# A two-layer trunk with adaLN on one core: where small loads are queued, at what rate modulation weights are taken in, how norm sums and reciprocals are formed, and what the weight splits queue behind

## The chip, the cores and the metric

One core of a Trainium2 chip runs the whole program. Its engines are TensorE (PE), VectorE (DVE), ScalarE (ACT), GpSimd (POOL) and SyncE (SP). The metric is the device time of one execution in microseconds, as the median of several. Every time below is of the kernel before the change.

## The reference

x is one sequence of 256 tokens with 2048 features, c one conditioning vector of 2048. For each of two layers:

```python
mod = (silu(c) @ ada_w[layer] + ada_b[layer])[:, None, :]          # 2048 -> 6 x 2048
sh_m, sc_m, g_m, sh_f, sc_f, g_f = jnp.split(mod, 6, axis=-1)
hm = rms_norm(x, norm_mix_g[layer]) * (1.0 + sc_m) + sh_m
y = ab_mixer(hm, ...) if layer == 0 else cd_mixer(hm, ...)         # each: one projection in, two mixers, one out
x = x + (1.0 + g_m) * y
hf = rms_norm(x, norm_ffn_g[layer]) * (1.0 + sc_f) + sh_f
x = x + (1.0 + g_f) * swiglu(hf, w_gate, w_up, w_down)             # 5632 wide
```

ab_mixer is a gated MLP over token chunks beside a state space scan (SSD) with a short convolution and a gated RMS norm. cd_mixer is stick-breaking attention on 12 heads beside block attention (MoBA) on 4 heads whose q and k get an RMS norm per head. All is in fp32.

## The kernel before

All activations lie transposed: 128 features on the partitions, 256 tokens along a row, 16 such k-tiles. Weights are streamed once, in slabs of two k-tiles by 512 columns (512 KB): SP issues the transfer of raw (L293, four buffers), ACT rounds it to hi (L295), DVE takes lo = raw - hi (L298), three buffers each. PE multiplies in fp32r three times: h by hi, l by hi, h by lo, where h and l are the same split of the activations. dense_ws (L315) keeps the weights stationary and moves 256 columns (the tokens), dense_as (L351) keeps the activations stationary and moves 512. The product of a whole block of 512 output columns gathers in PSUM (accps).

The modulation c @ ada_w is not made on PE. ada_unit (L194) brings in tiles of ada_w (araw, three buffers, L232; the first 16 tiles are in other buffers), and DVE multiplies each by a column of silu(c) and adds it into acc (L211). Behind the last tile end() sums acc over the partitions by small sel matmuls (L217, recorded at L156) and adds the bias (mod, L220). pump (L272) is called once per slab: it adds a rate (RATES for the three groups below, RATE after) and issues a tile for each whole unit. take (L266) makes the uses of tiles issued some slabs earlier.

The first stage, the projection of layer 0, runs in three groups over k: k-tiles 0 to 3, 4 to 8 and 9 to 15 (GROUPS), each over the same 14 blocks of 512 columns, so 28, 42 and 56 slabs. A group needs the modulation of its own k-tiles only. The first group's modulation is 16 tiles of 128x1024 that are read before any weight. What a group needs is made by gains (gs, L465) and adaln, per k-tile: t on DVE (L457), h on ACT (L459), l on DVE (L460). In the last group each finished block goes on to the convolution, the SSD or the gating (DVE and ACT).

At the start x comes in four tiles; PE turns them (L507), ACT copies them to xT (L508) and sums their squares (L515); the variance goes through a square root on ACT (L404) and a reciprocal of 128x2 on DVE (L405), and two matmuls with the reciprocal as a broadcast operand spread it over all partitions (L408). ACT also issues the small loads (rows of gains, biases and of SSD parameters, L126 to L137, L562, L563, L567), which PE then turns into columns (to_cols).

At the four later norms (before the SSD output, before both FFNs, before layer 1) Ssq gathers squares, total() sums them over the partitions by matmuls with one column (ones), and rstd_bcast (L399) does root, reciprocal and broadcast, with WARM matmuls on ident ahead and behind. Two of the norms, and the start, copy the result from PSUM (keep, L414); the others read it there. The eight MoBA norms (L943 to L950) go the same way without WARM.

The order on each engine comes from a scheduler that goes by priorities (tc.high_priority) and its own timeline; tc.issue_after binds one instruction behind another.

## Time and profile before

| | us |
|---|---|
| Three executions | 2680.24, 2683.21, 2684.34 |
| Median | 2683.21 |
| Profiled execution | 2682.86 |
| Its span in the trace | 2681.1 |
| PE busy (97% of the span) | 2610.5 |
| DVE busy (69%) | 1860.3 |
| ACT busy (46%) | 1235.4 |

A PE that is busy 97% of the span can still run at half clock, and its matmuls overlap in the records. So one reads the granted clock beside the busy time, stretch by stretch, and at each place where PE waits looks for what released it.

### The profile page before, as it was taken

The page shows a single profiled execution, that of the slowest core. Times are in us where ns is not written, and L with a number is a line of the kernel's source. Part 1 is how long each engine was busy: PE and PEld are TensorE (multiplying, and loading weights), DVE is VectorE, ACT ScalarE, POOL GpSimd, SP SyncE. Part 2 cuts the span into 40 slices and gives each one's busy share as a digit, 9 for nine tenths or more (in the row PEclk, how much of TensorE's full clock was granted, in tenths as well). Part 3 has the DMA queues.
Part 4 walks back from the last instruction along what each step waited for, and adds up shares of the span by engine and source line. Part 5 has one row for each costly group of instructions (what it writes and reads, how often), then busy time and mean ns, then how long its engine had stood idle before and what let it go on. Part 6 is the DMA issues. An engine that isn't in the chain of part 4 may idle for free.

```text
span 2681.1 us, 39012 instructions
## 1 busy us (share of the span) xinstructions
PE 2610.5 (97%) x15277; PEld 2301.9 (86%) x15277; DVE 1860.3 (69%) x2085; ACT 1235.4 (46%) x1540; POOL 3.2 (0%) x18
## 2 busy tenths in 40 slices
PE   4989999999999999999999999999999999999999
PEld 4989889999988888888888988999988888888888
DVE  5688997887867788777777777666655454445444
ACT  3533574654445444444444544444444444444443
POOL 0000000000000000000000000000000000000000
PEclk7999999999999999999999999999999999999999
DMA  7988797777879989999988788877466666666664
GB/s 269 294 283 304 235 300 253 214 244 232 294 246 306 307 291 307 305 305 301 302 299 301 227 280 283 277 246 230 152 195 189 189 192 188 189 188 191 189 194 144
DMA packets 303650, 665.79 MB, mean 248 GB/s; under 512 B 23504, under 2 KB 25962, under 8 KB 303466
## 3 DMA queue, kind: packets, MB, share of 16 engines
q1 hardware_dynamic: 300480, 662.79, 77.0%
q8 instruction: 119, 1.95, 0.3%
q10 hardware_dynamic: 2986, 0.51, 0.1%
q14 instruction: 65, 0.53, 0.1%
HBM read 661.12 MB, written 2.10 MB: 247 GB/s over the span
## 4 chain that ended last, share of the span: by engine, by line
PE 92%; DVE 3%; DMA 3%; issue 1%; ACT 1%; SPq 0%; ACTq 0%; DVEq 0%
PE accps L156 57%; PE accps L342 25%; PE pm L156 4%; PE pm L342 4%; PE pm L147 1%; DMA raw<-in_ab_w_in 1%; DMA araw<-in_ada_w 1%; DVE acc L211 1%; DVE lo L298 1%; DVE t L625 0%; ACT hi L295 0%; DVE t L457 0%; DMA t<-in_gm_w_s 0%; DMA blk<-in_x 0%; DMA blk<-in_ada_w 0%
## 5 line engine op out<-in xcount | busy, mean ns | idle before, releaser
L298 DVE TENSOR_TENSOR lo<-raw,hi 128x1024 fp32r<-128x1024 f32 (+1 forms) x878 | 1059.0, 1207 | 696.9 <-ACT hi L295 691.7
L295 ACT ACTIVATE hi<-raw 128x1024 fp32r<-128x1024 f32 (+1 forms) x878 | 917.8, 1046 | 1249.5 <-PE accps L156 817.2
L156 PE MATMUL accps<-hi,h 128*128 128x512 f32 x1664 | 651.1, 391 | 0.6 <-ACT hi L295 0.6
L156 PE MATMUL accps<-hi,l 128*128 128x512 f32 x1664 | 648.6, 390 | 2.3 <-DVE l L460 2.3
L342 PE MATMUL accps<-h,lo 128*128 128x256 f32 x1856 | 503.6, 285 | 7.3 <-DVE lo L298 7.3
L342 PE MATMUL accps<-h,hi 128*128 128x256 f32 x1856 | 504.9, 286 | 5.8 <-ACT h L459 5.2
L342 PE MATMUL accps<-l,hi 128*128 128x256 f32 x1856 | 503.9, 286 | 1.1 <-DVE l L389 0.6
L211 DVE SCALAR_TENSOR_TENSOR acc<-araw,ct,acc 128x1024 f32<-128x1024 f32 (+2 forms) x377 | 465.7, 1235 | 3.8 <-DMA araw<-in_ada_w 3.4
L156 PE MATMUL accps<-lo,h 128*128 128x512 f32 x1664 | 445.9, 390 | 0.4 <-DVE lo L298 0.4
L156 PEld LDWEIGHTS accps<-hi,l 128*128 128x128 f32 x1664 | 312.5, 188 | 67.1 <-DVE l L460 3.2
L156 PEld LDWEIGHTS accps<-hi,h 128*128 128x128 f32 x1664 | 312.5, 188 | 66.2 <-ACT hi L295 1.4
L156 PEld LDWEIGHTS accps<-lo,h 128*128 128x128 f32 x1664 | 311.8, 188 | 66.1 <-DVE lo L298 1.6
L342 PEld LDWEIGHTS accps<-h,hi 128*128 128x128 f32 x1856 | 348.2, 193 | 8.8 <-ACT h L459 6.0
L342 PEld LDWEIGHTS accps<-h,lo 128*128 128x128 f32 x1856 | 346.4, 193 | 10.5 <-DVE lo L298 8.9
L342 PEld LDWEIGHTS accps<-l,hi 128*128 128x128 f32 x1856 | 347.7, 193 | 3.0 <-DVE l L389 0.8
L156 PE MATMUL accps<-hi,blk 128*128 128x512 f32 x1248 | 310.3, 390 | 0.0
L156 PEld LDWEIGHTS accps<-hi,blk 128*128 128x128 f32 x1248 | 233.0, 188 | 47.7
L156 PE MATMUL accps<-lo,blk 128*128 128x512 f32 x624 | 166.9, 389 | 0.0
L156 PEld LDWEIGHTS accps<-lo,blk 128*128 128x128 f32 x624 | 117.1, 188 | 24.4
L342 PE MATMUL pm<-blk,hi 128*128 128x256 f32 x448 | 80.6, 284 | 0.0
L342 PE MATMUL accps<-blk,hi 128*128 128x256 f32 x384 | 69.7, 285 | 0.9 <-ACT blk L388 0.5
L342 PEld LDWEIGHTS pm<-blk,hi 128*128 128x128 f32 x448 | 69.3, 192 | 0.2
(238 smaller groups left out, 1538.7 us busy)
## 6 DMA issues: line engine op xcount, KB each, us to landing
araw<-in_ada_w SPq DMA_DIRECT2D x323, 512.0 KB, 5.4
raw<-in_ffn_w_gate SPq DMA_DIRECT2D x176, 512.0 KB, 4.2
raw<-in_ffn_w_up SPq DMA_DIRECT2D x176, 512.0 KB, 4.5
raw<-in_ffn_w_down SPq DMA_DIRECT2D x176, 512.0 KB, 4.9
raw<-in_ab_w_in SPq DMA_DIRECT2D x130, 512.0 KB, 4.9
raw<-in_cd_w_in SPq DMA_DIRECT2D x96, 512.0 KB, 4.7
raw<-in_ab_w_out SPq DMA_DIRECT2D x64, 512.0 KB, 5.0
raw<-in_cd_w_out SPq DMA_DIRECT2D x32, 512.0 KB, 4.7
```

The costliest lines, as they stand in the source:

```text
L147: T.transpose(dst, src, ident)
L156: return T.matmul(o, a, b, start=first, stop=last, skip_group_check=True)
L211: V.scalar_tensor_tensor(acc, r, ct[nr][:, g:g + 1], acc, op0=OP.mult, op1=OP.add)
L295: A.activation(hi, raw, AF.Copy)
L298: wlast[1] = V.tensor_tensor(lo, raw, hi.bitcast(F32), op=OP.subtract)
L342: T.matmul(acc[n], a[:, n * P:(n + 1) * P], b, start=first and n % 2 == 0, stop=final, skip_group_check=True)
```

## The change

There are six edits. First, ACT issues four small loads at its very front (c twice, the first layer's ada_b, the gains of the mixer norms) and the other small loads, with the narrow weight of dt, are issued by SP behind the first four slabs; their columns are made in block 4 of the first group. Second, RATES is 1.3, 0.92 and 0.3 in place of 0.9, 0.85 and 0.5, and QUIET leaves out the modulation tiles for 8 slabs behind the first adaln of a stage, except in the first stage. Third, rstd_of replaces total and rstd_bcast: matmuls with ones as a 128x128 operand give the sum on all partitions for 256 tokens, and root and reciprocal run on 128x256; the start keeps the old way. WARM goes, except at the start. Fourth, pace: the hi of slab i queues behind the h of k-tile 2i - 1, its lo behind the l of that tile; and each t queues behind the l two tiles ahead of it. Fifth, the tail blocks of dense_ws gather their last two columns tiles in PSUM tiles of their own. Sixth, dense_as makes all h by hi, then l by hi, then h by lo of a slab.

```diff
-WARM = (2, 2, 10)
-RATES = (0.9, 0.85, 0.5)
+QUIET = 8
+RATES = (1.3, 0.92, 0.3)
...
+        nc.scalar.dma_start(rows3[0:96, :], ada_b[0].rearrange("(k p) -> k p", p=P))
+        nc.scalar.dma_start(rows3[96:128, :], norm_mix_g.rearrange("l (k p) -> (l k) p", p=P))
...
+    def load_rows():
+        nc.sync.dma_start(rows1[32:64, :], rowview(norm_ffn_g))
...
+        nc.sync.dma_start(hb[:, 0, :], ssd_dt_bias.partition_broadcast(P))
+        nc.sync.dma_start(hb[:, 1, :], ssd_a_log.partition_broadcast(P))
...
     def pump():
         slab[0] += 1
+        if quiet[0]:
+            quiet[0] -= 1
+            return
...
+            after = pace[2 * npace[0] - 1] if 0 < 2 * npace[0] <= len(pace) else None
+            npace[0] += 1
             hi = stg.tile([P, 1024], F32R, tag="hi", name="hi", bufs=3)[:, 0:nk * ncol]
-            A.activation(hi, raw, AF.Copy)
+            with (tc.issue_after(after[0]) if after else ExitStack()):
+                A.activation(hi, raw, AF.Copy)
...
-            acc = [t[:, i * S:(i + 1) * S] for t in (pm(), pm()) for i in range(2)]
+            two = pm()
+            acc = [two[:, 0:S], two[:, S:2 * S], pm()[:, 0:S], pm()[:, 0:S]]
...
-            for part in range(2):
+            for part in range(3):
...
+                        dense_mm[0] = mm(acc[:, n, :], (bl if part == 1 else bh)[:, cs], (lo if part == 2 else hi)[:, i, :],
...
+    def rstd_of(sqs, scale):
+        ps = pm()
+        for i, t in enumerate(sqs):
+            mm(ps[:, 0:S], ones, t, first=(i == 0), last=(i == len(sqs) - 1))
+        r = tmp.tile([P, S], F32, tag="rb", name="rb", bufs=2)
+        A.activation(r, ps[:, 0:S], AF.Sqrt, bias=eps6, scale=scale)
         V.reciprocal(r, r)
...
+        return r
...
     def adaln(k, rb, gs, sh):
         t = t1()
-        V.scalar_tensor_tensor(t, xt(k), gs, rb, op0=OP.mult, op1=OP.mult)
+        with (tc.issue_after(pace[-2][1]) if len(pace) > 1 else ExitStack()):
+            V.scalar_tensor_tensor(t, xt(k), gs, rb, op0=OP.mult, op1=OP.mult)
...
-        nc.scalar.dma_start(wdt, w_in0[:, DT0:DT0 + HB].rearrange("(k p) n -> p k n", p=P))
+        nc.sync.dma_start(wdt, w_in0[:, DT0:DT0 + HB].rearrange("(k p) n -> p k n", p=P))
```

ACT at the start, from the last Square or the last evictions on to the first h. rs is the root, cols and adab are turned rows, rb the spread reciprocal. Before:

```order
L181 ACTIVATE t1_303<-t1_91 64x32 x4
L135 DMA t1_103<-in_ssd_conv_w 96x128
L143 ACTIVATE cols1_242<-pm_240 128x128
L136 DMA t1_103<-in_ssd_conv_b 24x128
L143 ACTIVATE adab0_246<-pm_244 128x128
L137 DMA t1_104<-in_ada_b 96x128
L563 DMA hb_351<-in_ssd_a_log 128x32
L567 DMA t2_2455<-in_ab_w_in 128x16x32
L404 ACT_TABLE_LOAD
L404 ACTIVATE rs_267<-var0_248,eps6_97 128x2
L416 ACTIVATE rb_273<-pm_270 128x256
L295 ACTIVATE hi_388<-raw_386 128x1024
```

Now:

```order
L506 ACTIVATE t2_280,half_265<-blk_137 128x512
L498 ACTIVATE xT1_128<-pm_200 128x512
L498 ACTIVATE xT1_128<-pm_206 128x512
L498 ACTIVATE xT2_129<-pm_212 128x512
L498 ACTIVATE xT2_129<-pm_218 128x512
L510 ACT_TABLE_LOAD
L510 ACTIVATE rs_283<-var0_264,eps6_104 128x2
L498 ACTIVATE xT3_130<-pm_224 128x512
L498 ACTIVATE xT3_130<-pm_230 128x512
L143 ACTIVATE adab0_262<-pm_260 128x128
L516 ACTIVATE rb_289<-pm_286 128x256
L295 ACTIVATE hi_367<-raw_365 128x1024
```

The five loads between the evictions and the root are gone from there, and the root stands ahead of the last two evictions of xT.

DVE at the end of group 0, around the mod of the second group (acc 128x640 is the second group's sum, acc 128x896 the third's). Before:

```order
L211 SCALAR_TENSOR_TENSOR acc_416<-araw_1242,ct2_298,acc_416 128x640
L298 TENSOR_TENSOR lo_1365<-raw_1361,hi_1363 128x512
L211 SCALAR_TENSOR_TENSOR acc_416<-araw_1245,ct2_298,acc_416 128x640
L211 SCALAR_TENSOR_TENSOR acc_416<-araw_1248,ct2_298,acc_416 128x640
L211 SCALAR_TENSOR_TENSOR acc_416<-araw_1251,ct2_298,acc_416 128x640
L209 TENSOR_SCALAR acc_1254<-araw_1255,ct2_298 128x896
L220 SCALAR_TENSOR_TENSOR mod0_0_112<-pm_1257,adab0_246 128x5
L220 SCALAR_TENSOR_TENSOR mod0_1_113<-pm_1257,adab0_246 128x5
L465 TENSOR_TENSOR gs_0_1_4_1266<-mod0_1_113,cols1_242 128x5
L457 SCALAR_TENSOR_TENSOR t1_1268<-xT1_125,gs_0_1_4_1266,rb_273 128x256
L457 SCALAR_TENSOR_TENSOR t1_1274<-xT1_125,gs_0_1_4_1266,rb_273 128x256
```

Now:

```order
L300 TENSOR_TENSOR lo_1214<-raw_1210,hi_1212 128x1024
L202 TENSOR_SCALAR acc_1127<-araw_1128,ct2_241 128x896
L300 TENSOR_TENSOR lo_1249<-raw_1245,hi_1247 128x1024
L204 SCALAR_TENSOR_TENSOR acc_1127<-araw_1163,ct2_241,acc_1127 128x896
L213 SCALAR_TENSOR_TENSOR mod0_0_115<-pm_1199,adab0_262 128x5
L300 TENSOR_TENSOR lo_1316<-raw_1312,hi_1314 128x1024
L213 SCALAR_TENSOR_TENSOR mod0_1_116<-pm_1199,adab0_262 128x5
L204 SCALAR_TENSOR_TENSOR acc_1127<-araw_1196,ct2_241,acc_1127 128x896
L454 TENSOR_TENSOR gs_0_1_4_1279<-mod0_1_116,adab0_262 128x5
L445 SCALAR_TENSOR_TENSOR t1_1281<-xT1_128,gs_0_1_4_1279,rb_289 128x256
L445 SCALAR_TENSOR_TENSOR t1_1287<-xT1_128,gs_0_1_4_1279,rb_289 128x256
```

Before, the last uses of the second group's tiles stand directly ahead of its mod; now two uses of the third group's tiles and slabs of the first group stand there, and h and l of the tiles come between slabs.

DVE at the second norm, from the last residual to the first l. Before:

```order
L791 SCALAR_TENSOR_TENSOR xT3_127<-pm_7955,mod0_2_114,xT3_127 128x256 x2
L298 TENSOR_TENSOR lo_8327<-raw_8323,hi_8325 128x1024
L211 SCALAR_TENSOR_TENSOR acc_6611<-araw_7934,ct2_298,acc_6611 128x1024
L298 TENSOR_TENSOR lo_8348<-raw_8344,hi_8346 128x1024
L405 RECIPROCAL rs_8229<-rs_8229 128x2
L211 SCALAR_TENSOR_TENSOR acc_6611<-araw_7986,ct2_298,acc_6611 128x1024
L457 SCALAR_TENSOR_TENSOR t1_8254<-xT0_124,gs_0_4_0_8252,pm_8232 128x256
L457 SCALAR_TENSOR_TENSOR t1_8260<-xT0_124,gs_0_4_0_8252,pm_8232 128x256
L457 SCALAR_TENSOR_TENSOR t1_8266<-xT0_124,gs_0_4_0_8252,pm_8232 128x256
```

Now:

```order
L793 SCALAR_TENSOR_TENSOR xT3_130<-pm_7931,mod0_2_117,xT3_130 128x256
L793 SCALAR_TENSOR_TENSOR xT3_130<-pm_7932,mod0_2_117,xT3_130 128x256
L407 RECIPROCAL rb_8198<-rb_8198 128x256
L445 SCALAR_TENSOR_TENSOR t1_8215<-xT0_127,gs_0_4_0_8213,rb_8198 128x256
L445 SCALAR_TENSOR_TENSOR t1_8221<-xT0_127,gs_0_4_0_8213,rb_8198 128x256
L448 SCALAR_TENSOR_TENSOR l0_8218<-t1_8215,mod0_3_118,h0_8217 128x256
L445 SCALAR_TENSOR_TENSOR t1_8227<-xT0_127,gs_0_4_0_8213,rb_8198 128x256
L448 SCALAR_TENSOR_TENSOR l1_8224<-t1_8221,mod0_3_118,h1_8223 128x256
L445 SCALAR_TENSOR_TENSOR t1_8233<-xT0_127,gs_0_4_0_8213,rb_8198 128x256
L300 TENSOR_TENSOR lo_8286<-raw_8282,hi_8284 128x1024
```

The reciprocal is the one on 128x256 and stands directly behind the residual; the uses of modulation tiles are gone from there, and l comes behind the second t.

## Rows read from the trace of the kernel before

**Rows 1.** The page: the engines' busy time, share and instructions; and the group of the weight split's lo on DVE (busy us, mean ns | idle before).

```profile
PE 2610.5 (97%) x15277; PEld 2301.9 (86%) x15277; DVE 1860.3 (69%) x2085; ACT 1235.4 (46%) x1540; POOL 3.2 (0%) x18
...
L298 DVE TENSOR_TENSOR lo<-raw,hi 128x1024 fp32r<-128x1024 f32 (+1 forms) x878 | 1059.0, 1207 | 696.9 <-ACT hi L295 691.7
```

**Rows 2.** Windows of 50 us of the core: length, busy us of PE, PEld, DVE, ACT and POOL (instructions), granted clock, DMA share, GB/s.

```profile
0.00:50.00 50.00, 17.52 (x67) 12.42 (x67) 22.36 (x27) 16.58 (x40) 3.15 (x18) 0.75 0.84 287
100.00:150.00 50.00, 40.94 (x279) 38.82 (x277) 33.38 (x43) 21.21 (x26) 0.00 (x0) 0.90 0.83 271
200.00:250.00 50.00, 50.00 (x353) 46.79 (x352) 47.17 (x48) 18.65 (x20) 0.00 (x0) 1.00 0.98 346
300.00:350.00 50.00, 46.06 (x268) 40.17 (x268) 50.00 (x84) 29.91 (x48) 0.00 (x0) 0.97 0.78 240
400.00:450.00 50.00, 46.47 (x383) 44.87 (x383) 40.68 (x56) 19.21 (x24) 0.00 (x0) 1.00 0.79 251
```

**Rows 3.** The waits of PE over the span: engine, tile and line <- what it waited for: us in total, times, longest us.

```profile
PE pm L156 <- DVE rs L405: 18.0, 1, 18.0
PE pm L156 <- DVE acc L211: 10.2, 2, 6.9
```

**Rows 4.** Timeline of ACT and its queue (ACTq issues transfers): start us, us, what [idle before <- releaser].

```profile
10.71 2.07 ACT L508 ACTIVATE xT<-pm 128x512 f32<-128x512 f32 x4 [6.82 <-DMA t<-in_moba_k_norm_g]
...
26.80 0.32 ACTq L135 DMA_DIRECT2D t<-in_ssd_conv_w  x1
...
29.52 0.32 ACTq L136 DMA_DIRECT2D t<-in_ssd_conv_b  x1
...
30.87 0.32 ACTq L137 DMA_DIRECT2D t<-in_ada_b  x1
...
33.85 0.40 ACTq L567 DMA_DIRECT2D t<-in_ab_w_in  x1
34.28 1.28 ACT L404 ACT_TABLE_LOAD   x1 [4.12 <-DMA raw<-in_ab_w_in]
```

**Rows 5.** Timeline of DVE, and below it of PE, up to the first dense matmul: start us, us, what [idle before <- releaser].

```profile
35.90 0.17 DVE L405 RECIPROCAL rs<-rs 128x2 f32<-128x2 f32 x1 [13.16 <-ACT rs L404]
35.98 2.60 DVE L211 SCALAR_TENSOR_TENSOR acc<-araw,ct,acc 128x1024 f32<-128x1024 f32 x2
38.62 7.89 DVE L211 SCALAR_TENSOR_TENSOR acc<-blk,ct,acc 128x1024 f32<-128x1024 f32 x6
...
46.66 3.54 PE L156 MATMUL pm<-ones,acc 128*128 128x1 f32 x16 [3.23 <-DVE acc L211]
...
52.18 1.22 PE L342 MATMUL accps<-h,hi 128*128 128x256 f32 x4 [1.45 <-ACT h L459]
```

**Rows 6.** The chain that ended last, in order of time, at three places: start us, us, what (DMA: from issue to landing).

```profile
15.02 7.70 DMA araw<-in_ada_w
...
128.22 4.49 DMA araw<-in_ada_w
...
137.15 5.83 DMA araw<-in_ada_w
...
242.08 5.98 DMA araw<-in_ada_w
```

**Rows 7.** The page's DMA issues: transfer, queue and operation, count, KB each, median us from issue to landing.

```profile
araw<-in_ada_w SPq DMA_DIRECT2D x323, 512.0 KB, 5.4
```

**Rows 8.** Timeline of all engines at the end of group 0 (SPq: SP's queue): start us, us, what [idle before <- releaser].

```profile
136.24 1.92 DVE L211 SCALAR_TENSOR_TENSOR acc<-araw,ct,acc 128x640 f32<-128x640 f32 x2
137.15 7.11 SPq L232 DMA_DIRECT2D araw<-in_ada_w  x4
...
140.72 2.30 PE L156 MATMUL pm<-sel,acc 128*128 128x2 f32 x10 [6.92 <-DVE acc L211]
...
145.15 1.22 PE L342 MATMUL accps<-h,hi 128*128 128x256 f32 x4 [2.13 <-ACT h L459]
```

**Rows 9.** Windows of three other stretches, columns as in rows 2.

```profile
138.00:149.00 11.00, 6.15 (x30) 6.06 (x31) 6.08 (x16) 2.10 (x5) 0.00 (x0) 0.53 0.71 237
755.00:760.00 5.00, 5.00 (x16) 2.88 (x16) 3.51 (x4) 0.65 (x2) 0.00 (x0) 0.66 0.73 192
1540.00:1570.00 30.00, 30.00 (x234) 29.11 (x233) 21.30 (x24) 14.97 (x24) 0.00 (x0) 1.00 0.85 282
```

**Rows 10.** Timeline of ACT and PE at the second norm: start us, us, what [idle before <- releaser].

```profile
754.12 0.71 ACT L435 ACTIVATE t<-xT 128x256 f32<-128x256 f32 x2
...
759.62 0.38 ACT L416 ACTIVATE rb<-pm 128x256 f32<-128x256 f32 x1 [3.69 <-PE pm L156]
...
761.11 0.49 PE L156 MATMUL accps<-hi,h 128*128 128x512 f32 x1
...
762.92 0.50 PE L156 MATMUL accps<-hi,l 128*128 128x512 f32 x1 [1.32 <-DVE l L460]
```

**Rows 11.** Durations on DVE by line and form: ns min/median/max, first and last start us, forms.

```profile
L405 DVE RECIPROCAL rs<-rs x13: 156/163/168, 35.9 to 1931.6; 128x2 f32<-128x2 f32 x13
...
L591 DVE RECIPROCAL t<-t x1: 542/542/542, 278.2 to 278.2; 128x64 f32<-128x64 f32 x1
...
L457 DVE SCALAR_TENSOR_TENSOR t<-xT,gs,pm x40: 472/476/482, 760.0 to 1946.4; 128x256 f32<-128x256 f32 x40
```

**Rows 12.** Timeline of PE at the fourth norm: two matmuls of 512 columns on ident, each in two passes.

```profile
1933.33 1.88 PE L156 MATMUL pm<-ident 128*128 128x512 f32 x4
```

More of the change, by code (lines that the diff above doesn't have):

```diff
@@ L156, in mm @@
         return T.matmul(o, a, b, start=first, stop=last, skip_group_check=True)
-    def warm(n, after):
-        with tc.issue_after(after.ins):
-            ps = pm()
-            for t in n if isinstance(n, list) else [ident[:, None, :].to_broadcast([P, 4, P])] * n:
-                mm(ps, ident, t)
     ct, sel = {}, {}
@@ L309, in trunk @@
     later = deque()
+    dense_mm = [None]
     def run_later():
@@ L341, in dense_ws @@
             for n, (a, b, first, final) in order:
-                T.matmul(acc[n], a[:, n * P:(n + 1) * P], b, start=first and n % 2 == 0, stop=final,
-                         skip_group_check=True)
+                dense_mm[0] = T.matmul(acc[n], a[:, n * P:(n + 1) * P], b, start=first and (n % 2 == 0 or n > pair),
+                                       stop=final, skip_group_check=True)
             if done >= min(DEFER, len(ks)):
@@ L395, in xt @@
         return xT[k // 4][:, k % 4, :]
-    bcast = [None]
-    def rstd_bcast(var, eps, scale, after=None):
-        if after is not None:
-            warm(WARM[0], after)
-        r = small(2, "rs")
-        A.activation(r, var, AF.Sqrt, bias=eps, scale=scale)
-        V.reciprocal(r, r)
-        ps = pm()
-        for cc in range(2):
-            last = mm(ps[:, cc * P:(cc + 1) * P], r[:, cc:cc + 1].to_broadcast([P, P]), ident, first=(cc == 0))
-        bcast[0] = last
-        if after is not None:
-            warm(WARM[1], last)
-        return ps[:, 0:S]
-    def keep(rb):
-        t = tmp.tile([P, S], F32, tag="rb", name="rb", bufs=2)
-        A.activation(t, rb, AF.Copy)
-        return t
+    def rstd_of(sqs, scale):
[4 more added lines that the diff above has]
+        A.activation(r, ps[:, 0:S], AF.Sqrt, bias=eps6, scale=scale)
+        V.reciprocal(r, r)
+        return r
     def warm_sqrt(ssq):
@@ L517, in trunk, with later_cols @@
         V.tensor_reduce(var0, half.rearrange("p (c i) -> p c i", c=2), axis=AX.X, op=OP.add)
-        rb0 = keep(rstd_bcast(var0, eps6, 1.0 / D))
-        warm(firsts[WARM[2]:], bcast[0])
-        take()
-    more_cols()
-    load_rows_b()
-    cols2 = to_cols(rows2, "cols2")
-    adab[1] = to_cols(rows4, "adab1")
+        r0 = small(2, "rs")
+        A.activation(r0, var0, AF.Sqrt, bias=eps6, scale=1.0 / D)
+        V.reciprocal(r0, r0)
+        psr = pm()
+        for cc in range(2):
+            last = mm(psr[:, cc * P:(cc + 1) * P], r0[:, cc:cc + 1].to_broadcast([P, P]), ident, first=(cc == 0))
+        rb0 = tmp.tile([P, S], F32, tag="rb", name="rb", bufs=2)
+        A.activation(rb0, psr[:, 0:S], AF.Copy)
+        with tc.issue_after(last.ins):
+            psw = pm()
+            for t in firsts[10:]:
+                mm(psw, ident, t)
+        take()
+    cols = {}
+    def later_cols():
+        with tc.issue_after(dense_mm[0].ins):
+            cols[1] = to_cols(rows1, "cols1")
+            cols[2] = to_cols(rows2, "cols2")
+            adab[1] = to_cols(rows4, "adab1")
     w_in0 = ab_w_in[0]
```

108 lines of the change are left out of this document (48 added, 60 removed).

## The prediction

> **What bounds the kernel now.** I read the page first: PE is busy 2610.5 us of the span of 2681.1 us [rows 1]. The profiled execution took 2682.86 us, 1.8 us more than its span, and lies 0.35 us under the median of the three, so the sum below is made against 2682.86. An edit can gain only where PE stands or runs at a lower clock. The windows of 50 us say where that is [rows 2]: from 0 to 50 PE is busy 17.52 us, from 100 to 150 it is busy 40.94, and 300:350 and 400:450 lose 3.94 and 3.53 while DVE is at 50.00 and 40.68. A window such as 200:250 loses nothing, with DVE at 47.17 and 346 GB/s moved. The waits of PE name the largest releasers [rows 3]: 18.0 us for one reciprocal and 10.2 us for acc. Then I went to each place.
>
> **Start.** ACT's program order is the cause. Five small loads stand ahead of its square root; each is issued only when a transfer ahead of it has landed, so that the first of these issues is at 26.80 and the last at 33.85; then come 1.28 us of table load and the root [rows 4]. DVE's reciprocal waits for that, 13.16 us idle, and behind it in DVE's order stand eight uses of the modulation weights that had landed: 2.60 + 7.89 = 10.5 us. Only then come the sel matmuls at 46.66 (3.54 us) and the first dense matmul at 52.18 [rows 5].
> In the changed order the loads on ACT are four and at the very front, and the root stands behind the squares and six of the evictions. ACT makes its first evictions at 10.71 [rows 4]. Six evictions (0.52 each, 2.07 for four), eight Squares of the same width at 0.6, the table load and the root end by 20 us even one behind the other from there, and nearer to 16 if the Squares begin as each x tile lands. DVE runs at 1.30 us per use, so the 13 uses behind the reciprocal need 16.9 us. Of the 16 weights the ninth landed at 15.02 + 7.70 = 22.7 [rows 6]; the stream's landings are 1.35 us apart (estimate from ACT's issues at 29.52 and 30.87, which each follow one), so the last lands at about 32.2. DVE ends at 33.5 (bound by landings) to 37 (by its own work). The sel matmuls take 3.5, and from there to the first dense matmul it took 52.18 - 50.20 = 2.0. That gives 39 to 42.5; I take 39, because the root's inputs are there long before the last weight. That is **-13 us** (-9 to -15). Two things can take some back: the SSD row that the exponential on ACT needs is now the tenth small load on SP, and that exponential stands ahead of h3; the narrow weight of dt stands ahead of the hi of the fourth slab. The four first slabs land by 32.2 + 4 x 1.35 = 37.6; issued behind these, both loads land at some 44 to 49 us, with 5.4 us to landing as a large one has [rows 7], which is when PE gets to them. I add nothing and leave 3 us in the range.
>
> **End of group 0.** PE runs out of work at 140.72 - 6.92 = 133.8 [rows 8] (28 slabs since 52.18, so 2.9 us each), and the chain there is araw transfers of 4.49 and 5.83 us one behind the other, with a few uses between [rows 6]. Then come the sel matmuls at half clock (2.30 us) and the wait for h (2.13); dense work resumes at 145.15. So the hole is 11.35 us, and the clock, 0.53 in 138:149 [rows 9], is low for some 3 us behind it, which costs half of that. At a rate of 1.3 per slab in place of 0.9, all 32 transfers of group 1's modulation are issued by slab 28 and its sel matmuls stand two slabs ahead of the end of group 0. Each use costs DVE 0.96 us (1.92 for two [rows 8]) and lies under a slab of 2.9 us on PE beside one lo of 1.21 [rows 1]: 1.21 + 1.3 x 0.96 = 2.46. The four transfers issued in a row took 7.11 us [rows 8], or 1.78 each, and 1.3 of them 2.3 us: less than a slab too. Then only the sel matmuls (half of 2.30 at full clock) and a part of the wait for h remain: **-10 us** (0 to -11.5; the upper end is what a slower stream leaves, below).
>
> **End of group 1 and the stretch to 420.** There one araw transfer of 5.98 us [rows 6] ends the wait, and t and h follow; PE idles some 2.5 us and has a stretch at half clock. With group 2's sel matmuls four slabs ahead that is -4. Behind it DVE is full (300:350: 50.00 [rows 2]). Eight narrow uses of 0.96 have gone ahead into group 0, and at 0.3 per slab in place of 0.5 five fewer wide ones of 1.30 stand in group 2: 14 us less DVE work behind 145, where PE lost 7.5 us in the two windows named. I count well under half of this, because the waits are also for conv and for a late weight of the spatial part: -3. Together **-7** (0 to -12).
>
> **The four norms.** Now: matmuls to one column, root, a reciprocal of 2 columns, a broadcast matmul, and a copy out of PSUM at two of them; PE is filled with matmuls on ident. At the second one the last Square ends at 754.83, the first dense matmul is at 761.11 and the next waits 1.32 us for l, until 762.92 [rows 10]. After: five matmuls of 256 columns, root and reciprocal on 128x256. What a reciprocal on 128x256 costs no row shows. The rows give 162 ns at 2 columns and 542 ns at 64 [rows 11]; the line through both gives 1.72 us at 256, and the lower bound is 0.48 us, what t (also 128x256) takes [rows 11]. I take 1.7, since the 64-column row already shows that the time grows with the columns. A sum matmul costs at most 0.47 (two of 512 columns take 1.88 [rows 12]). From the last Square: 0.47 + root 0.4 (a copy of this shape from PSUM is 0.38 [rows 10]) + 1.7 + t 0.48 + h 0.55 = 3.6 us to the first matmul, against 761.11 - 754.83 = 6.3 now at the second. The others gain less: no copy out of PSUM lies in the chain of the third and fourth, and at the first the root followed on other work. But l now comes right behind the second t, so the wait for l shrinks. Against that stands the clock: without matmuls on ident PE idles 3 us. With them the clock still fell at the second norm (0.66 in 755:760 [rows 9]). I take **-2** in all (-8 to +5, with the upper end at 1.75 us more for each).
> The Trainium skill, page "TensorE: Matmul & The Clock Gate", Part 1, says that the throttled clock is the default state and that activity releases it, which speaks against dropping the matmuls on ident; the window of the second norm shows that they did not hold the clock there. By the rule the sum is rival 3's.
>
> **MoBA heads.** Eight norms: PE saves the broadcast and two thin sums for one 256-column matmul, about 0.45 us each (estimate: it drops two thin sums and two of 128 columns, and adds one of 256 at 0.47), -3.6. DVE pays 8 x 1.5 = 12 us; in 1540:1570 it is busy 21.30 of 30 [rows 9], so 8.7 of the 12 fit there and the rest must find room in the slabs around: **-2** (+3 to -4). The new order in dense blocks, the slabs queued behind operands and the eight slabs without modulation I count at 0 (+-3): the next stages show no PE wait that they could remove.
>
> Sum: -13 - 10 - 7 - 2 - 2 = -34. 2682.86 - 34 = **2649 us**.
>
> **Rivals.**
> 1. *The stream cannot feed 1.3 per slab.* A slab is 524 KB and 1.3 narrow transfers are 426 KB: 950 KB in 2.9 us are 327 GB/s. The trace has moved 346 in 200:250, but 287 in 0:50 and 271 in 100:150 [rows 2]. At 287 a slab takes 3.31 us, 28 slabs lose 11.5: the gain at group 0's end is spent inside it, 2660.
> 2. *The start gains issue time only.* If the root then waits for the same landings, what is saved is five issues of 0.32 to 0.40 us [rows 4], 1.7 us in place of 13: 2660. Against it: nothing in the root's inputs comes from these loads. The Trainium skill, page "DMA: Bandwidth & Descriptors", section "Issuing engines are not separate DMA queues", says just this of starting DMAs on several engines: they end on the same 16 DMA engines and only the issue time is saved. The rows show a queue of ACT's that holds compute behind an issue, which the rule doesn't speak of.
> 3. *Cold norms.* Half clock at all four norms for about 3.5 us each, as at 755:760, costs 1.75 x 4 = 7: 2656.
> 4. *Slower: araw stalls the weights.* Araw issues stand between raw issues on SP, and uses between lo's on DVE, each in order. With three buffers one transfer goes through per third of a buffer's turn: landing 5.4 us in the median [rows 7] + use 0.96 = 6.4, so 2.1 us each and 1.3 of them 2.8 per slab: this is just under PE's 2.9. It decides from there on. If many in flight make a landing 9.5 us, a turn is 10.5, a slab 4.5 us, and 28 slabs lose 46 us: 2649 + 46 = 2695. It passes "no change" at a loss of 34 us, 4.1 us per slab, a landing of 8.5 us. For it: 1.78 us each is what four issues in a row showed, but with few raw transfers beside. Against it: the transfers that were waited for there took 4.49 and 5.83 us [rows 6], not 8.5.
>
> **How the numbers follow.** Forecast 2649: 0.60 (its own range 2634 to 2657). Rival 1: 0.12, rival 2: 0.06, rival 3: 0.10; all these are faster: 0.88. Rival 4: 0.12, of which 0.05 end within 0.2% (5.4 us, about what a measurement of this kernel can tell from no change) and 0.07 beyond it. The range goes from 2632 (start -15, hole -11.5, stretch -12, norms -8, MoBA -4 would be -50; all of them together is unlikely) to 2668 (rivals 1 or 2 with 8 us of the bounds of norms and MoBA); outside lie rival 4 and a small part at the lower end.
>
> **What would show it.** Right: the first dense matmul near 39 us and no DVE idle over 5 us before it; PE busy over 47 of 50 us in 100:150; sel matmuls of group 1 between dense matmuls; PE waits for acc under 2 us in all; a reciprocal of about 1.7 us on 128x256. Wrong: a first dense matmul past 45; lo waits on PE in the first 28 slabs with DVE waiting for araw (rivals 1 and 4: told apart by whether the DMA share is near 1); granted clock of 0.5 after each norm (rival 3); PE waiting for lo beside the MoBA reciprocals.

## The result, and the profile after

The median of four executions is 2646.49 us (2643.51 to 2647.96), against 2683.47 for the kernel before: the ratio is 0.9863, with a 95% interval from 0.9846 to 0.988. That is 37 us; forecast were 34. The profiled execution took 2643.51 us with a span of 2641.8. It is the fastest of the four, so a difference read between two traces need not be the one between the medians: the two spans differ by 39.3 us.

The page gives PE less busy time than in [rows 1], since part of the half clock and the matmuls on ident behind the norms are gone:

```profile
PE 2586.1 (98%) x15141; PEld 2284.4 (86%) x15141; DVE 1876.6 (71%) x2085; ACT 1241.7 (47%) x1538; POOL 3.1 (0%) x19
```

The windows of 50 us, to be held against [rows 2] (columns as there):

```profile
0.00:50.00 50.00, 28.08 (x134) 20.79 (x135) 32.59 (x47) 21.00 (x47) 3.06 (x19) 0.83 0.87 299
100.00:150.00 50.00, 50.00 (x420) 50.00 (x419) 44.58 (x53) 23.95 (x29) 0.00 (x0) 1.00 0.93 317
300.00:350.00 50.00, 48.75 (x257) 40.19 (x255) 43.77 (x72) 40.89 (x74) 0.00 (x0) 1.00 0.83 262
```

From 0 to 50 PE has 10.6 us more, and from 100 to 150 the 9.1 us of the hole are back, with DVE at 44.58 in place of 33.38. In 300:350 PE still loses, but 1.25 us in place of 3.94.

The waits of PE (us in total, times, longest) answer to [rows 3]:

```profile
PE accps L348 <- DVE lo L300: 11.7, 12, 3.1
PE pm L156 <- DMA blk<-in_ada_w: 8.2, 2, 8.0
PE accps L156 <- ACT h L447: 6.8, 2, 3.4
...
PE accps L348 <- ACT h L447: 5.2, 2, 3.4
PE accps L348 <- ACT h L391: 3.4, 1, 3.4
...
PE pm L156 <- DVE acc L204: 0.5, 1, 0.5
```

The two large waits of before are gone: the one for the reciprocal at the start, and acc fell from 10.2 us to 0.5. What is on top now is lo (DVE's load in the third group), a wait at the start for weights that nothing useful waits for, and h, 3.4 us at each of the four norms. (The row left out is a wait of 5.9 us in PE's first work; it was 4.0 before.)

The start, as timelines of ACT, DVE and PE, answers to [rows 4, 5]:

```profile
16.76 0.30 ACT L510 ACTIVATE rs<-var,eps 128x2 f32<-128x2 f32 x1
...
17.30 5.24 DVE L204 SCALAR_TENSOR_TENSOR acc<-blk,ct,acc 128x1024 f32<-128x1024 f32 x4
...
26.53 7.89 DVE L204 SCALAR_TENSOR_TENSOR acc<-blk,ct,acc 128x1024 f32<-128x1024 f32 x6
...
32.95 1.13 PE L156 MATMUL pm<-blk,ident 128*128 128x512 f32 x2 [0.24 <-DMA blk<-in_ada_w]
34.57 1.92 PE L156 MATMUL pm<-ones,acc 128*128 128x1 f32 x16 [0.49 <-DVE acc L204]
38.23 1.22 PE L348 MATMUL accps<-h,hi 128*128 128x256 f32 x4 [1.75 <-ACT h L447]
```

The root is at 16.76, right behind the evictions, and from 17.30 on DVE makes its 13 uses (4, then 3 on araw, then 6) without a gap until 34.43: DVE's own work ends this chain. The landings are close behind: PE's filler on the last tile waits for it until 32.95, and one use of 1.3 us behind that would have ended at 34.25. The sel matmuls took 1.92 us at full clock (3.54 before, at half), and the first dense matmul is at 38.23, not at 52.18.

At the end of group 0 the chain (start us, us, what) has no transfer left in it, where [rows 6] had one after the other:

```profile
99.95 17.16 PE accps L348 x143
117.11 1.01 PE pm L156 x10
118.12 6.94 PE accps L348 x57
```

The sel matmuls stand between dense ones. The first dense matmul of the second group is at 123.82; before it was at 145.15 [rows 8].

The second norm, as timelines of PE and DVE, answers to [rows 10], and the new reciprocal to [rows 11]:

```profile
724.95 1.89 PE L156 MATMUL pm<-t,ones 128*128 128x256 f32 x8
...
727.38 1.75 DVE L407 RECIPROCAL rb<-rb 128x256 f32<-128x256 f32 x1 [1.75 <-ACT rb L406]
729.17 0.88 DVE L445 SCALAR_TENSOR_TENSOR t<-xT,gs,rb 128x256 f32<-128x256 f32 x2
730.23 0.48 DVE L448 SCALAR_TENSOR_TENSOR l<-t,mod,h 128x256 fp32r<-128x256 f32 x1 [0.18 <-ACT h L447]
...
730.25 2.08 PE L156 MATMUL accps<-hi,h 128*128 128x512 f32 x4 [3.41 <-ACT h L447]
```

```profile
L407 DVE RECIPROCAL rb<-rb x12: 1693/1744/1753, 627.8 to 1892.3; 128x256 f32<-128x256 f32 x12
```

The reciprocal takes 1744 ns; the line through 2 and 64 columns had given 1720. From the beginning of the sums to the first dense matmul pass 5.3 us. l is there with the second dense matmul, so that nothing is waited for behind it.

Where the time came from, read off the two traces at the same points of the program:

| point | before | after | shift |
|---|---|---|---|
| first dense matmul | 52.18 | 38.23 | -13.95 |
| first of the second group | 145.15 | 123.82 | -21.33 |
| first norm, sums begin | 653.11 | 624.88 | -28.23 |
| first norm, dense again | 659.10 | 630.61 | -28.49 |
| second norm, sums | 752.71 | 724.95 | -27.76 |
| second norm, dense again | 761.11 | 730.25 | -30.86 |
| third norm, sums | 1506.60 | 1475.49 | -31.11 |
| third norm, dense again | 1514.61 | 1480.80 | -33.81 |
| fourth norm, sums | 1928.31 | 1889.91 | -38.40 |
| fourth norm, dense again | 1934.65 | 1895.22 | -39.43 |
| end of the span | 2681.1 | 2641.8 | -39.3 |

So some seven tenths come by the first norm, and from one of these points to the next the shift never shrinks by more than 0.7 us.

### The profile page after: what moved, and what is told of

Its sections match the earlier page's. It is cut to its first block, busy times and chain, and to the rows that moved or that the text cites. A ratio compares the mean times of both kernels' runs of the same rounds, so it can differ in the third digit from the quotient of the medians.

```text
span 2641.8 us, 38711 instructions
## 1 busy us (share of the span) xinstructions
PE 2586.1 (98%) x15141; PEld 2284.4 (86%) x15141; DVE 1876.6 (71%) x2085; ACT 1241.7 (47%) x1538; POOL 3.1 (0%) x19
## 4 chain that ended last, share of the span: by engine, by line
PE 93%; DVE 4%; DMA 2%; issue 1%; ACT 1%; SPq 0%; ACTq 0%; DVEq 0%
PE accps L156 58%; PE accps L348 25%; PE pm L348 4%; PE pm L156 4%; PE pm L147 1%; DVE acc L204 1%; DVE lo L300 1%; DVE t L627 1%; DMA araw<-in_ada_w 0%; DMA raw<-in_ab_w_in 0%; DMA blk<-in_ada_w 0%; DVE rb L407 0%; DMA t<-in_gm_w_s 0%; ACT hi L295 0%; DVE blk L475 0%
## 5 line engine op out<-in xcount | busy, mean ns | idle before, releaser
L156 PE MATMUL accps<-hi,h 128*128 128x512 f32 x1664 | 450.8, 392 | 6.9 <-ACT h L447 6.8
L156 PE MATMUL accps<-hi,l 128*128 128x512 f32 x1664 | 446.7, 390 | 0.0
```

Of the source, the lines that this page charges most:

```text
L156: return T.matmul(o, a, b, start=first, stop=last, skip_group_check=True)
```

## The experiments

Each row below gives the median of four or five executions; the kernel before, run on the same chip beside them, was at 2683.21 (first four runs), 2682.19 (next four) and 2682.57 (last four), the changed kernel at 2646.49 with 2683.47 beside it. Where a difference to the changed kernel is told, it holds these 1.3 us of drift; the executions of one kernel lie between 1.1 us (rate_01) and 7.4 us (old_norms) apart, and differences under 3 us are not told apart. The fifth edit, the tail's PSUM tiles, was taken back only together with the norms and in loads_only; no run has it alone.

| run | us | ratio to before, interval |
|---|---|---|
| loads_only | 2672.23 | 0.9959 [0.9946, 0.9973] |
| old_rates | 2659.57 | 0.9912 [0.9898, 0.9925] |
| old_norms | 2648.09 | 0.9868 [0.9855, 0.9882] |
| old_moba | 2651.10 | 0.9881 [0.9868, 0.9895] |
| no_pace | 2658.28 | 0.9909 [0.9896, 0.9923] |
| old_dense | 2648.35 | 0.9871 [0.9858, 0.9885] |
| warm_new | 2641.42 | 0.9846 [0.9833, 0.986] |
| rate_01 | 2636.56 | 0.9829 [0.9815, 0.9842] |
| no_quiet | 2653.05 | 0.9889 [0.9872, 0.9905] |
| rate_18 | 2650.24 | 0.9881 [0.9866, 0.9895] |
| combo_a | 2632.94 | 0.9813 [0.9799, 0.9828] |
| combo_b | 2631.92 | 0.9812 [0.9797, 0.9826] |

**The loads alone.** The changed kernel with all other edits taken back.

```diff
-RATES = (1.3, 0.92, 0.3)
+RATES = (0.9, 0.85, 0.5)
-QUIET = 8
+QUIET = 0
 # norms, MoBA heads, dense_as, tail and the queueing of hi, lo and t as in the kernel before
```

> Of the six edits only the first is made: the small loads leave ACT's queue; rates, norms, MoBA heads, order of the weight splits and of dense blocks are as before. Theory (the root was held behind ACT's load issues): the first dense matmul at about 38 us as in the changed kernel, 11 us of the 14 kept by the 24th slab, the two holes at the ends of groups 0 and 1 still there: 2672 (2669 to 2676). Rival (only issue time is saved): 2681. Rival (the start is given back in the stretch where DVE is full): first dense matmul early, but 2678 to 2683.

Measured: 2672.23, 11.0 us under before and in the theory's band. The timeline of PE:

```profile
38.27 1.22 PE L343 MATMUL accps<-h,hi 128*128 128x256 f32 x4 [1.96 <-ACT h L476]
...
130.79 2.30 PE L156 MATMUL pm<-sel,acc 128*128 128x2 f32 x10 [8.33 <-DVE acc L204]
```

The first dense matmul is where the changed kernel has it, and the hole for acc is still there, earlier by 10 us. Counted from the kernel before, the nth lo on DVE is 11.3 us early at the 24th slab and between 9.0 and 12.0 us early at all later ones. So nothing is given back later, and the rival by which only issue time is saved falls: five issues would have been 1.7 us. The Trainium skill, page "DMA: Bandwidth & Descriptors", section "Issuing engines are not separate DMA queues", says that starting transfers on several engines saves only the issue time. This case shows 11.0 us beside it, because the issuing engine had a root behind its issues; whether the transfers themselves gain is not shown.

**The rates taken back.**

```diff
-RATES = (1.3, 0.92, 0.3)
+RATES = (0.9, 0.85, 0.5)
```

> The changed kernel with the rates 0.9, 0.85, 0.5 of before. Theory (the hole at the end of group 0 is araw tiles that come too late): PE waits again for acc at the end of group 0 (about 11 us with the low clock behind it) and for t and h at the end of group 1 (4 us): 2661 (2657 to 2666). Rival (the new order of t, h, l and the slabs closes the holes, the rates are not needed): PE waits for acc under 3 us, 2648 to 2650. Rival (the high rate costs the slabs of group 0 something): the body of group 0 is faster by some 3 us than in the changed kernel, 2658.

Measured: 2659.57, 13.1 us more than with the change and in the theory's band. The hole is back, as a timeline of PE shows:

```profile
129.14 2.29 PE L156 MATMUL pm<-sel,acc 128*128 128x2 f32 x10 [5.89 <-DVE acc L204]
```

The new order of t, h, l and slabs didn't close it; the rate does. The other half of the theory missed: at the end of group 1 PE waits for nothing in this run (200 to 260), where before it waited 1.6 us for h and 0.5 for l, so the old rates don't bring that hole back.

**The four norms as before.**

```diff
-            return rstd_of([self.acc] + self.tail, 1.0 / D)
+            ps = pm()
+            ts = [self.acc] + self.tail
+            for i, t in enumerate(ts):
+                for cc in range(2):
+                    last = mm(ps[:, cc:cc + 1], t[:, cc * P:(cc + 1) * P], ones[:, 0:1], ...)
+            return rstd_bcast(ps[:, 0:2], eps6, 1.0 / D, last)
```

> The changed kernel with the four norms of before (one-column sums, root and reciprocal of two columns, broadcast matmuls, matmuls on ident, the tail's PSUM tiles as before). Theory: from the shift between the two traces at the slabs around each norm the new ones gave +0.5, -3.4, 0 and -2.4 us, so 2652 (2649 to 2655). Rival (cold norms: the half clock behind three of the new norms eats what they save): 2644 to 2647. In the old form the clock should stay at full speed behind the first norm.

Measured: 2648.09, between the two bands, and within its scatter (2643.78 to 2651.22) not told apart from the changed kernel: 1.6 us by the medians. Between the two traces, each with three stretches of low clock of 3.4 us at norms, this run is longer by 4.1 us (spans 2645.9 and 2641.8). So the old form costs between nothing and some 4 us here; which, these runs don't settle. From the first sum to the first dense matmul the second norm now takes 6.04 us, where the changed kernel takes 5.30:

```profile
726.19 0.95 PE L156 MATMUL pm<-ones,t 128*128 128x1 f32 x8
...
732.23 1.19 PE L156 MATMUL accps<-hi,h 128*128 128x512 f32 x4
```

The clock still fell at three of the four norms in this run (the first, third and fourth), in spite of the matmuls on ident, which the expectation had not foreseen for the first norm.

**The MoBA norms as before.**

```diff
-            rb = rstd_of([sq], 1.0 / P)
+            ps = pm()
+            for cc in range(2):
+                mm(ps[:, cc:cc + 1], sq[:, cc * P:(cc + 1) * P], ones[:, 0:1], first=(cc == 0))
+            rb = rstd_bcast(ps[:, 0:2], eps6, 1.0 / P)
```

> The changed kernel with the eight MoBA norms of before. Theory (PE saves a broadcast and two thin sums for one 256-column matmul, 0.45 us per head): 2650. From the shift between the traces over these slabs, 6 us: 2652. Rival (eight reciprocals of 1.74 us on DVE delay lo's, so that the old form is as fast): 2645 to 2647.

Measured: 2651.10, 4.6 us more; between the two traces 3.7 us come over these slabs. One head's broadcast and thin sums take PE 0.61 and 0.50 us in this run (at 1548.57). The two windows of 90 us over the eight heads, of this run and then of the changed kernel, have PE busy without a break and DVE at 65.04 and 75.86:

```profile
1520.00:1610.00 90.00, 90.00 (x484) 77.89 (x484) 65.04 (x79) 41.68 (x56) 0.00 (x0) 1.00 0.82 271
```

```profile
1517.00:1607.00 90.00, 90.00 (x458) 76.95 (x457) 75.86 (x82) 45.02 (x60) 0.00 (x0) 1.00 0.86 285
```

So DVE takes the 12 us of reciprocals without making PE wait, and the price per head is PE's alone: 4.6 / 8 = 0.57 us by the medians.

**Without the queueing and the pauses.**

```diff
-QUIET = 8
+QUIET = 0
-        with (tc.issue_after(pace[-2][1]) if len(pace) > 1 else ExitStack()):
-            V.scalar_tensor_tensor(t, xt(k), gs, rb, op0=OP.mult, op1=OP.mult)
+        V.scalar_tensor_tensor(t, xt(k), gs, rb, op0=OP.mult, op1=OP.mult)
 # hi and lo likewise, apart from the lo's of the first group
```

> The changed kernel without the new queueing: no hi, lo or t bound behind operand tiles (only the first group's lo's behind the last l, as before), and no 8 slabs without modulation tiles. The runs so far leave 37 - 11.0 (loads) - 13.1 (rates) - 4.6 (MoBA) - 1.6 (norms) = 6.7 us unexplained. Theory (the queueing keeps l next to t, so that the wait for l at the norms, 1.32 and 0.98 us before, goes, and with it some low clock): 2651 (2648 to 2654), with waits for l back at the second and fourth norm. Rival (worth nothing, as the prediction counted it): 2645 to 2648. Rival (the pauses shorten transfers' backlog and are worth all): 2653 or more.

Measured: 2658.28, 11.8 us more: above the first two bands and in the last, whose reason (the pauses are worth all) the next run takes away. The timelines of PE and DVE at the second norm show what comes back:

```profile
729.21 0.59 PE L156 MATMUL pm<-t,ones 128*128 128x256 f32 x2
...
729.81 1.22 DVE L296 TENSOR_TENSOR lo<-raw,hi 128x1024 fp32r<-128x1024 f32 x1
730.94 1.28 DVE L204 SCALAR_TENSOR_TENSOR acc<-araw,ct,acc 128x1024 f32<-128x1024 f32 x1
732.14 1.22 DVE L296 TENSOR_TENSOR lo<-raw,hi 128x1024 fp32r<-128x1024 f32 x1
733.27 1.28 DVE L204 SCALAR_TENSOR_TENSOR acc<-araw,ct,acc 128x1024 f32<-128x1024 f32 x1
734.47 1.75 DVE L403 RECIPROCAL rb<-rb 128x256 f32<-128x256 f32 x1
...
737.33 2.07 PE L156 MATMUL accps<-hi,h 128*128 128x512 f32 x4 [5.04 <-ACT h L442]
```

Two lo's and two modulation uses now stand in front of the reciprocal in DVE's order, and PE waits 5.04 us for h in place of 3.41. The low clock there lasts 6.8 us, 3.8 of them on dense matmuls; in the changed kernel it is 3.4 and 2.9. Over the four norms it lies on dense work for 17 us in this trace and for 10 in the changed kernel's. At half speed the 7 us more can cost up to 4 of the 11.8 us.

**Only the pauses taken back.**

```diff
-QUIET = 8
+QUIET = 0
```

> The changed kernel with the queueing kept, but without the 8 slabs that leave out modulation tiles behind a norm. Together both were worth 11.8 us. Theory (most of it is the queueing: lo's and modulation uses stood ahead of the reciprocal and of t, and slabs behind the norm's own order): 2647 to 2650. Rival (the pauses: a modulation use of 1.28 us beside t, t, l, l and lo makes DVE the limit of the slabs behind the norm, 3.14 + 0.8 us against 2.9): 2653 to 2658.

Measured: 2653.05, 6.6 us more, in the rival's band; the theory's number fell. DVE's timeline in the slabs behind the second norm:

```profile
735.48 1.22 DVE L300 TENSOR_TENSOR lo<-raw,hi 128x1024 fp32r<-128x1024 f32 x1
736.61 1.28 DVE L204 SCALAR_TENSOR_TENSOR acc<-araw,ct,acc 128x1024 f32<-128x1024 f32 x1
...
739.39 1.22 DVE L300 TENSOR_TENSOR lo<-raw,hi 128x1024 fp32r<-128x1024 f32 x1
```

In each slab a use of 1.28 us follows the lo, and two t and two l stand behind it: 739.39 - 735.48 = 3.91 us from lo to lo, where PE needs 2.7 per slab (12 matmuls of 512 columns at 0.227) and the changed kernel's DVE took 2.72 (lo's at 731.82 and 734.54). But PE waits for none of it here: from 728 to 775 its one wait is the 3.41 us for h, as in the changed kernel. It waits behind the third norm, three times for l:

```profile
PE accps L348 <- DVE l L448: 2.1, 3, 0.8
```

That is 2.1 of the 6.6 us. Another part can be clock: at the norms it is low on dense work for 16 us here and for 10 in the changed kernel's trace. The rest was not located. By these two runs the pauses are worth 6.6 us, and the queueing, tried without them, the other 5.2 of the 11.8.

**The order in dense_as.**

```diff
-            for part in range(3):
+            for part in range(2):
 # h by hi and l by hi alternate again, h by lo last
```

> The changed kernel with the order of before in dense_as: h and l by hi alternating, then h by lo. Both give a lo four matmuls by eight of time. Theory (no PE wait in these blocks to remove): 2645 to 2648. Rival (the three runs of one weight kind save PE time): the cadence of a 512-column matmul in the FFN blocks changes from 0.227 us and the time by 2 us or more.

Measured: 2648.35, not told apart from the changed kernel. The median cadence of a 512-column matmul is 227 ns in both traces, so the rival's sign is absent.

**Matmuls on ident behind the sums.**

```diff
+        if len(sqs) > 1:
+            with tc.issue_after(last.ins):
+                pw = pm()
+                for i in range(3):
+                    mm(pw, ident, ident[:, None, :].to_broadcast([P, 4, P]))
```

> The changed kernel with three 512-column matmuls on ident put behind the sums of each of the four norms (about 2.6 us of the 3.4 in which PE idles there). Theory (the clock's fall behind three norms, 3.4 us at half each, is not tied to the idle PE, since the rows before show it with such matmuls too): falls at one to three norms still, 2644 to 2648. Rival (idle PE costs the clock): full clock behind all norms and 1.7 us saved at each of three, 2641.

Measured: 2641.42. My theory fell, the rival was right. Windows of 5 us from the first dense matmul on, at the four norms of the changed kernel and then of this run (granted clock is the first number behind POOL):

```profile
630.00:635.00 5.00, 4.39 (x22) 4.17 (x23) 5.00 (x15) 2.89 (x8) 0.00 (x0) 0.66 0.15 54
730.00:735.00 5.00, 4.75 (x15) 3.82 (x16) 4.82 (x11) 4.25 (x8) 0.00 (x0) 0.68 0.14 27
1480.00:1485.00 5.00, 4.20 (x23) 4.20 (x24) 4.82 (x11) 4.21 (x7) 0.00 (x0) 0.66 0.06 7
1895.00:1900.00 5.00, 4.78 (x21) 3.89 (x22) 4.82 (x11) 4.26 (x8) 0.00 (x0) 1.00 0.16 25
```

```profile
633.00:638.00 5.00, 3.99 (x31) 3.79 (x32) 5.00 (x15) 3.33 (x8) 0.00 (x0) 1.00 0.11 43
732.00:737.00 5.00, 4.75 (x21) 3.92 (x22) 4.82 (x11) 4.25 (x8) 0.00 (x0) 1.00 0.14 20
1481.00:1486.00 5.00, 4.54 (x36) 4.34 (x37) 4.82 (x11) 4.25 (x8) 0.00 (x0) 1.00 0.12 18
1894.00:1899.00 5.00, 4.31 (x19) 3.51 (x20) 4.82 (x12) 4.22 (x7) 0.00 (x0) 1.00 0.10 14
```

The clock fell behind three norms and now behind none. The 5.1 us between the medians (3.8 with the drift of the kernel before taken off) look like three times the 1.7 that 3.4 us at half clock can cost, but that is luck in part: read at the same points of the two traces, the full clock gave back 0.8, 1.3 and 1.2 us behind the first three norms, 3.3 in all, and the spans, 2641.2 and 2641.8, differ by less because this run came to the first norm 2.8 us later. The medians also hold falls that the profiled execution of the changed kernel lacks: with the same norms old_dense, no_quiet, rate_01 and rate_18 show the clock falling behind all four.

**Fewer modulation uses in the third group.**

```diff
-RATES = (1.3, 0.92, 0.3)
-RATE = 0.62
+RATES = (1.3, 0.92, 0.1)
+RATE = 0.78
```

> The changed kernel with the third rate 0.1 in place of 0.3 and the later rate 0.78 in place of 0.62: some 11 uses of 1.28 us, 14 us of DVE work, leave the stretch from 220 to 400 where PE waits for lo (some 10 us in all). Theory (DVE's load in that stretch makes the waits): a third to a half goes, 2642 (2639 to 2645). Rival (the waits there are bursts of conv and SSD work that no rate changes): 2645 to 2648. Rival (the uses come back later where DVE is short too): 2648 or more.

Measured: 2636.56, 9.9 us less, more than expected. The window of 180 us over the third group's DVE work, in the changed kernel and in this run:

```profile
220.00:400.00 180.00, 168.69 (x1217) 156.67 (x1216) 165.40 (x255) 107.21 (x165) 0.00 (x0) 0.99 0.80 253
```

```profile
220.00:400.00 180.00, 174.78 (x1276) 165.32 (x1275) 157.31 (x248) 109.87 (x172) 0.00 (x0) 0.98 0.75 232
```

DVE has 8.1 us less and PE 6.1 us more. PE's waits for lo fell from 11.7 us to 6.9. Some of the slabs' lead is lost again later (10.6 us at the 158th slab, 5.8 at the 215th), as the last of its rivals had it, but the rest stays. Two rates were changed at once, so how much of the later course is the second one's is not shown.

**A still higher first rate.**

```diff
-RATES = (1.3, 0.92, 0.3)
+RATES = (1.8, 0.92, 0.3)
```

> The changed kernel with the first rate 1.8 in place of 1.3. Rival 4 of the prediction named the stream: a slab and 1.8 narrow tiles are 1114 KB in 2.9 us, 384 GB/s, more than the 355 of the changed kernel's busiest window, and DVE needs 1.22 + 1.8 x 0.88 = 2.8 us per slab. Theory (above what the stream can bring, the slabs wait): PE waits in group 0 for lo or hi, the body of group 0 is 4 to 10 us longer, 2650 to 2657. Rival (tiles simply come when they come, no slab waits): 2644 to 2648.

Measured: 2650.24. The number is in the theory's band, but not for its reason. Windows in group 0, of this run and of the changed kernel:

```profile
60.00:80.00 20.00, 20.00 (x162) 19.70 (x162) 16.37 (x17) 11.27 (x14) 0.00 (x0) 1.00 0.99 348
```

```profile
60.00:80.00 20.00, 20.00 (x161) 19.63 (x160) 16.35 (x17) 11.63 (x15) 0.00 (x0) 1.00 1.00 357
```

PE loses nothing in either. The DMA engines are full at 1.3 already (1.00 here, and 0.99 at 351 GB/s from 80 to 100), and a higher rate brings no more bytes: tiles come when they come, no slab is held up, and the 28th lo, the last of group 0, is 0.3 us from its place in the changed kernel. What is lost (3.7 us by the medians, 7.1 between the traces) is lost later, most of it between the 160th slab and the second norm. A part is clock, low for 6.8 us at each of the first two norms in place of 3.4; what loses the rest was not tried.

**Both gains together,** and once more with a smaller later rate.

```diff
 # warm_new and rate_01; combo_b has this in place of 0.78:
+RATE = 0.7
```

> The changed kernel with both edits that gained alone: three matmuls on ident behind the sums of each norm, third rate 0.1 and later rate 0.78. If the gains add up, 2646.5 - 5.1 - 9.9 = 2631.5 (2630 to 2634). Rival (part of the lower rate's gain was low clock at other places that the matmuls save too): 2634 to 2636.

> As the last, with the later rate 0.70 in place of 0.78, so that some of the uses move past the SSD stretch. In the run with 0.78 three of the 10 us came back between slabs 158 and 190, where DVE is short too. Theory: these come back less, 2629 to 2631. Rival (the modulation of the second half of the first FFN is then late): PE waits for acc or t near slab 270, 2633 or more.

Measured: 2632.94 and 2631.92. They beat both kernels: combo_b is 50.7 us under the kernel before, 0.9812 with an interval up to 0.9826. The two gains add up to 13.6 of 15.0 us, as the first expectation had it; 2631.92 lies between the two bands of the second, and between the two later rates nothing can be told. The clock is not safe in these runs: behind the first norm it fell again (0.50 in 628.10:631.40 of combo_a and in 626.50:629.80 of combo_b). There PE waited 1.59 and 3.27 us for h in spite of the matmuls on ident; behind the other three norms it waited 0.84 and the clock stayed.

## Why the prediction was right, and where it was not

**Start: right in place and price.** Forecast 39 us for the first dense matmul, measured 38.23. By itself the edit gives 11.0 us. The 3 us left in the range for small loads were used: the exponential waits for its row until 43.45, and h3 behind it in ACT's order, while PE runs at half clock until 43.7.

```profile
43.45 0.23 ACT L577 ACTIVATE hb<-hb 128x32 f32<-128x32 f32 x1 [2.23 <-DMA hb<-in_ssd_a_log]
43.59 0.49 ACT L447 ACTIVATE h<-t,mod 128x256 fp32r<-128x256 f32 x1
```

That 39 came so near is luck in part, since two misses cancel: I put DVE's end at 33.5, and it came at 34.43, where DVE's 13 uses in a row and the last landing (34.25 with one use) bound it almost alike; and I put the sel matmuls at 3.5 us, and at full clock they took 1.92.

**End of group 0: right.** -10 forecast; the body from the first dense matmul to the second group's first was 145.15 - 52.18 = 93.0 and is 123.82 - 38.23 = 85.6, which is 7.4 us, and the low clock behind it, worth some 1.6, is gone. Taking the rates back costs 13.1 us, of which this hole is the larger part. Rival 1, that the stream can't feed 1.3, was close to the truth in its size (the DMA engines are 0.99 busy at 351 to 357 GB/s, 327 were needed) and still didn't decide: the slabs didn't wait. Rival 4 needed landings of 8.5 us; in 40 to 120 us the medians were 5.1 for raw and 5.0 for araw, and even at 1.8 no slab of group 0 came late.

**End of group 1 and behind: right in sign, near in size.** From the second group's first matmul to the first norm the shift grew by 6.9 us (-21.33 to -28.23), with the low clock behind 145 in it; forecast were 7. The -4 for the end of group 1 has come, but it doesn't hang on the rates: PE waits for no h there with the old rates in the new order (old_rates), nor with the new rates in the old order (no_pace). For the stretch behind, rate_01 shows that DVE's modulation uses do hold PE here, and that the change left most of it: I counted less than half of that cover as loss, and the same lever, pulled further, gave 9.9 us more. A part is not a matter of rates: at 348.45 DVE stood idle 4.78 us for the transfer of a layer norm row, with lo's behind it in its order.

```profile
348.45 1.42 DVE L715 SCALAR_TENSOR_TENSOR blk<-blk,nmu,t 128x512 f32<-128x512 f32 x2 [4.78 <-DMA t<-in_gm_ln_g]
```

**The norms: the sum was right for the wrong reason.** The step that failed is "the new order in dense blocks, the slabs queued behind operands and the eight slabs without modulation I count at 0 (+-3): the next stages show no PE wait that they could remove". The rows of before did show one, in the 1.32 us for l that I had read [rows 10] and booked to the new form of the norm. Without queueing and pauses the changed kernel loses 11.8 us. The traces show how queueing and form hang together, by the time from the first sum to the first dense matmul:

| kernel | second norm | third | fourth | together |
|---|---|---|---|---|
| before | 8.40 | 8.01 | 6.34 | 22.75 |
| new form, old order, no pauses (no_pace) | 8.12 | 8.12 | 6.19 | 22.43 |
| old form, new order (old_norms) | 6.04 | 7.36 | 7.34 | 20.74 |
| both (changed kernel) | 5.30 | 5.31 | 5.31 | 15.92 |

The form alone gains 0.3 us, the order alone 2.0, and both 6.8. The reciprocal on 128x256 is as dear as forecast (1.74 us), and it pays only when nothing stands ahead of it in DVE's order. no_quiet has 5.30 at each of the three as well, so here it is the queueing, not the pauses. That the old form costs just 1.6 us by the medians doesn't contradict this: over all four norms it takes 6.5 us longer up to the first dense matmul, and behind three of the new norms the low clock takes 3.3 us back (warm_new).

**The clock: rival 3 was real, inside the forecast.** Half clock behind three of four norms in the profiled execution and behind all four in other runs with the same norms; warm_new took it out and gave back 3.3 us between the traces, 5.1 between the medians. The Trainium skill, page "TensorE: Matmul & The Clock Gate", Part 1, says that the throttled clock is the default and that activity releases it. The traces agree with that here: with 3.4 us of idle PE the clock fell behind three of four norms, and with 0.84 us it fell behind none. I had held against it that the clock fell at the second norm with matmuls on ident, and old_norms repeats that at the first, third and fourth: PE waited there for less than 1 us at any norm, and the clock fell at three. What I overlooked is where it fell. At the second norm of the kernel before:

```profile
756.00:759.00 3.00, 3.00 (x6) 1.36 (x5) 2.51 (x4) 0.00 (x0) 0.00 (x0) 0.50 0.91 210
```

From 759.5 to 761 the clock is 1.00 again, and dense work begins at 761.11: the low clock slows the matmuls on ident (3.37 us for two, where the first norm took 1.96) and the broadcast behind them, but no dense matmul. old_norms has it so at all three norms, and there a fall costs 1.3 us (7.36 and 7.34 us in the table above, 6.04 at the second norm, which has none). In the changed kernel it lies on dense matmuls (730:733 at 0.50, dense from 730.25). So the kernel before paid for the clock too, at two norms, and the change's own loss to it is smaller than rival 3's 7 us. Those older norms put one-column sums, ident matmuls and a broadcast in a row; warm_new has full-width sums and ident matmuls. Which of these operations let the clock fall stays open.

**MoBA: mis-sized.** -2 forecast, 4.6 measured by the medians: the loss on DVE that I set against PE's 3.6 didn't come.

**The sum.** The single prices (11.0 loads, 13.1 rates, 11.8 queueing and pauses, 4.6 MoBA, 1.6 norms, 1.9 dense_as) make 44.0, more than the 37 measured. An edit taken out of the changed kernel can cost more than it gives alone where another leans on it, as form and queueing do at the norms; but the last two prices are not told apart from nothing, and the scatter of the others can make a part of these 7 us too. How they divide between pairs of edits was not tried.

## What to carry to other kernels

An engine that issues transfers among its arithmetic holds the arithmetic whenever an issue has to wait; look for it where an engine is idle ahead of an operation whose inputs are long there, and move the issues to a queue that has no arithmetic. When a chain through one engine's order (here reciprocal, t, l on DVE) comes to the front, look at what else stands in that order together with the form of the chain's steps: here a better form behind old work gained 0.3 us at three norms, the work bound behind the old form 2.0, and both together 6.8. And fill the idle time of TensorE ahead of dense work, but only as far as the operands need: 2.7 us of matmuls on ident in 3.4 us of waiting kept the clock at all four norms and gave back 3 to 5 us. Then read the granted clock at each place, and where the low stretch lies: behind one-column sums the same matmuls on ident did not hold it.
